# A two-layer streaming encoder step on one core: elementwise work moved from GpSimd to VectorE

## Chip, cores and metric

One NeuronCore of a Trainium2 chip runs the whole program. The metric is the device time of one execution in microseconds (us). PE is the matrix engine TensorE, DVE is VectorE, ACT is ScalarE, POOL is GpSimd, and SP is the engine that issues nearly all loads and stores.

## What is computed

The reference is a two-layer trunk with width 1024, run over 1024 prompt frames and 64 sample frames. Layer 0 mixes tokens with causal pooling windows, layer 1 with the gated linear recurrence HGRN2. Each layer ends in a convolutional feed-forward block, and an RMS norm closes the trunk. The feed-forward block, to which most of the change belongs, is this:

```python
up = jnp.einsum('bld,df->blf', h, w_up)
gate_pre, val = jnp.split(up, 2, axis=-1)
ext = jnp.concatenate([hist.astype(up.dtype), gate_pre], axis=1)
conv = cb
for j in range(CONV_W):
    conv = conv + cw[j] * ext[:, j:j + L]
hid = jax.nn.silu(conv.astype(F32)) * val.astype(F32)
y = jnp.einsum('blf,fd->bld', hid.astype(h.dtype), w_down)
```

and the trunk ends with `x = rmsnorm(x, norm_out_g)`. All inputs and outputs are float32. The hidden width is 2816, that is 22 blocks of 128.

## The kernel before

**Tiling.** The 1088 columns (frames) are three chunks: 384, 384 and 256 + 64 (the last 64 are the sample). Activations lie with 128 features on the partitions and frames along the free axis. The running sum x of each chunk stays in SBUF.

**Each product is three matmuls.** PE multiplies in a rounded format (F32R). Each operand is split into a high part, rounded by ACT, and a low part, the difference of the original and the high part. `mm3` (L181 to L185) adds hi x hi, hi x lo and lo x hi in a PSUM bank. `load_ready` (L112 to L133) loads a weight block of 128x512 through SP into one of five "raw" buffers, rounds it on ACT (L131) and makes the low part (L132) on the engine that `lo_engine` (L109) names: DVE in the HGRN part, for the pooling weights and for the first blocks of each feed-forward part (up blocks 0 to 3, down blocks 0 and 1), POOL for all others. There are eight places for the pairs of high and low part; when PE's last use of a place is issued, `drop` frees it and the next block is loaded. A raw buffer is free when its low part is made.

**Feed-forward.** Its 22 hidden blocks are done in 11 groups of two. The first group is computed plainly. From the second group on, chunks 0 and 1 are multiplied in Strassen's manner: seven products instead of eight, on sums and differences of weight parts (L155, on DVE) and of activations (`sums`, L426, on DVE). `Block.part` (L700) takes one of the products "3", "4", "1", "5", "2", "7", "6" at a time, and collects them: the partial sum e, the gate rows ge0 and ge1, and the values v0. Product "7" holds two subtractions on POOL, L727 and L730. `conv` (L618) does the three taps (L632 on ACT, L633 and L634 on DVE, SiLU at L635 on ACT), `hidden` (L638) multiplies by the values and splits the result. Chunk 2 is computed plainly (`plain`, L664). In the last group the plain blocks of chunk 2 come at the end, with parts named "upp". `down` (L752) multiplies two hidden blocks with the down weights, one PSUM bank for each of 8 output blocks and three chunks, and adds each bank to x (L760, on DVE). The down stage of a group runs inside the next group. There are three PSUM banks for the up products of chunks and chains and five for all else.

**Final norm.** `norm` (L356) with kind 3 squares x on ACT, adds up the squares on DVE and POOL (L369), sums over the partitions with PE transposes, takes the reciprocal root by Newton steps on DVE (`rstd`, L332 to L348), spreads it back into a PSUM bank by PE, copies that bank on ACT (L401), and multiplies x by it (L408): for chunks 0 and 1 on POOL, for chunk 2 on DVE but for two of eight. SP stores the output in pairs of blocks.

**Order.** PE's instruction order is written by hand (`manual_schedule`, L1087): Python generators are run by a small planner (`run`, L264) with estimated costs. For the other engines the framework orders the instructions when it builds the program. POOL besides does copies of two columns and fills (L625 to L628, L682, L684, L689, L722, L729, L732, L1013).

Of the kernel before, what the change touches and what calls it, by code (L numbers as in the profile page):

```python
# [9 lines left out]
F32 = mybir.dt.float32  # L10
# [55 lines left out]
def trunk_kernel(ctx: ExitStack, tc: tile.TileContext, xtok, xs_tok, hist_tok, xf, par, gmix, pw, winm, ident_in,  # L66
                 masks_in, w_up, w_dn, w_in, w_out, s0, y_out, npool, nhg, nconv):
    nc = tc.nc
# [37 lines left out]
    free = [(i, False) for i in range(NR)]  # L106
    extra_w = []

    def lo_engine(ph, key):  # L109
        return nc.vector if ph == "g" or key[0] == "pw" or key[0] in ("up", "dn") and key[2] < (4, 2)[key[0] == "dn"] else nc.gpsimd  # L110

    def load_ready(most=None):  # L112

        while queue and (most is None or len(loaded) < most):
            ph, key, make = queue[0]
            own = [p for p in free if p[1]] if ph == "g" and key[:2] not in (("out", H - 2), ("out", H - 1)) else []
            p = own[0] if own else next((p for p in free if not p[1]), None)
            if p is None:
                return
            free.remove(p)  # L120
            queue.pop(0)
            places[key] = p
            i, extra = p
            nm = "_".join(str(k) for k in key)
            if extra:
                hi, lo = (extra_w[i // 2][:, (i % 2 * 2 + b) * HW_:(i % 2 * 2 + b + 1) * HW_] for b in range(2))
            else:
                hi = wp.tile([P, HW_], F32R, name=f"whi{nm}", tag=f"whi{i}", bufs=1)
                lo = wp.tile([P, HW_], F32R, name=f"wlo{nm}", tag=f"wlo{i}", bufs=1)
            src = make(nm)  # L130
            nc.scalar.copy(hi, src)  # L131
            lo_engine(ph, key).tensor_tensor(lo, src, hi.bitcast(F32), op=ALU.subtract)  # L132
            loaded[key] = (hi, lo)  # L133

    def raw_block(nm, src, i):
# [190 lines left out]
    def slot(nm, tag, bufs=1, dt=F32, w=SLOT):  # L326
        return wk.tile([P, w], dt, name=nm, tag=tag, bufs=bufs)
# [28 lines left out]
    def norm(c, gbase, nm, kind):  # L356
# [5 lines left out]
        for d in range(ND):  # L362
            a = acc[d % 2][:, :n]
            if d < 2:
                nc.scalar.activation(a, x[c][:, d, :], AF.Square)
            else:
                sq = slot(f"sq_{nm}{d}", *tags[2:])
                last = nc.scalar.activation(sq[:, :n], x[c][:, d, :], AF.Square)
                (nc.vector if kind < 3 or c == 2 or d % 2 else nc.gpsimd).tensor_tensor(a, a, sq[:, :n], op=ALU.add)  # L369
        if final:  # L370
            with tc.issue_after(last.ins):
                for d in range(ND):
# [23 lines left out]
            yield 0.0, L_ROWS  # L396
        if kind == 0 and c == 0:
            nc.scalar.copy(piece("r0", *T1[6 + c], F32), pr[:, :n])
        if final:
            rs = slot(f"r_{nm}", "cv", 3)  # L400
            nc.scalar.copy(rs[:, :n], pr[:, :n])  # L401
        while kind == 2 and c < 2 and not last_proj:
            yield 0.0, 0.2
        for d in range(ND):
            if final:
                on_pool = c < 2 or d in (2, 5)
                eng, r_ = (nc.gpsimd, rs) if on_pool else (nc.vector, pr)
                eng.tensor_tensor(x[c][:, d, :], x[c][:, d, :], r_[:, :n], op=ALU.mult)  # L408

                if c < 2 and d % 2 or c == 2 and (d % 2 == 0 or d == ND - 1):  # L410
                    d0 = d - (0 < d and (c < 2 or d % 2 == 0))
                    nc.sync.dma_start(y_out[c][:, d0:d + 1, :], x[c][:, d0:d + 1, :])
            else:
                if kind == 2 and c < 2 or kind == 0 and c == 1:
                    t = row(kind // 2, c, d)
                elif kind == 0 and c < 2:
                    t = slot(f"hn_{nm}{d}", ("hh1", "hl1")[d % 2], 2, F32, NMAX)
                else:
                    t = slot(f"hn_{nm}{d}", "cv", 3)
                last = nc.vector.scalar_tensor_tensor(t[:, :n], x[c][:, d, :], col(gbase, d), pr[:, :n], op0=ALU.mult, op1=ALU.mult)  # L420
                split(hn_hi[c][:, d, :], hn_lo[c][:, d, :], t[:, :n], nc.vector)
                if d < ND - 1:
                    yield 0.0, N_STEP[kind]
# [189 lines left out]
    def ffn(l, hn_ready, late_deps, gbase, nm, kind):  # L613
# [82 lines left out]
        class Block:  # L696
# [3 lines left out]
            def part(self, t, keep=False):  # L700
# [22 lines left out]
                elif t == "2":  # L723
                    self.v0 = kept(f"v{nm}", "v", 2, ps)
                elif t == "7":
                    g0 = slot(f"g{nm}", "g", 1)[:, :N0]
                    nc.gpsimd.tensor_tensor(g0, self.e, self.ge1[:, 2:2 + N0], op=ALU.subtract)  # L727
                    ge0 = slot(f"ge{nm}_0", "ge", 3)
                    nc.gpsimd.memset(ge0[:, 0:2], 0.0)  # L729
                    nc.gpsimd.tensor_tensor(self.e, self.e, self.v0, op=ALU.subtract)  # L730
                    nc.vector.tensor_tensor(ge0[:, 2:2 + N0], g0, ps[:, :N0], op=ALU.add)
                    nc.gpsimd.tensor_copy(self.ge1[:, 0:2], ge0[:, N0:N0 + 2])  # L732
                    hidden(j, jj, 0, conv(j, 0, ge0), self.v0, hid)
                else:
                    nc.vector.tensor_tensor(self.e, self.e, ps[:, :N0], op=ALU.add)
                    hidden(j, jj, 1, conv(j, 1, self.ge1), self.e, hid)
# [446 lines left out]
```

## Time and profile before

| what | value |
|---|---|
| median of 3 runs | 2343.5 us (2336.83 to 2346.57) |
| profiled execution, its own time | 2341.33 us |
| its span, first to last instruction | 2339.5 us |
| mean granted TensorE clock in it | 0.988 of full |
| PE busy | 2269.2 us, 97% |
| DVE busy | 1621.5 us, 69% |
| ACT busy | 904.5 us, 39% |
| POOL busy | 755.1 us, 32% |
| bytes from HBM | 210.51 MB |

All times in the profile are of one execution; the runs shown beside it lie within 0.5% of each other. The page gives busy time for each engine, and the views of the trace break it down by stretch, by line and by wait. A busy engine is not the bound by itself: what matters is whose work PE, or the end of the program, waits for.

### The profile page before, as it was taken

The page shows a single profiled execution, that of the slowest core. Times are in us where ns is not written, and L with a number is a line of the kernel's source. Part 1 is how long each engine was busy: PE and PEld are TensorE (multiplying, and loading weights), DVE is VectorE, ACT ScalarE, POOL GpSimd, SP SyncE. Part 2 cuts the span into 40 slices and gives each one's busy share as a digit, 9 for nine tenths or more (in the row PEclk, how much of TensorE's full clock was granted, in tenths as well). Part 3 has the DMA queues.
Part 4 walks back from the last instruction along what each step waited for, and adds up shares of the span by engine and source line. Part 5 has one row for each costly group of instructions (what it writes and reads, how often), then busy time and mean ns, then how long its engine had stood idle before and what let it go on. Part 6 is the DMA issues. An engine that isn't in the chain of part 4 may idle for free.

```text
span 2339.5 us, 38021 instructions
## 1 busy us (share of the span) xinstructions
PE 2269.2 (97%) x13830; PEld 2219.9 (95%) x13830; DVE 1621.5 (69%) x3926; ACT 904.5 (39%) x1965; POOL 755.1 (32%) x856
## 2 busy tenths in 40 slices
PE   9899999999999989999999999989999999999996
PEld 8899999999999989999999999889999999999996
DVE  7896665666666698767666767788665666665667
ACT  6444433333443353323223322344433333444335
POOL 0024555455564500000000000001455455655555
PEclk9999999999999999999999999999999999999998
DMA  7124333334433321001001100102433333443331
GB/s 244 43 95 136 117 123 121 118 120 134 136 113 130 123 69 37 26 19 55 27 28 48 33 27 22 37 30 86 130 114 131 118 123 121 139 132 118 125 114 78
DMA packets 118099, 218.70 MB, mean 93 GB/s; under 512 B 13436, under 2 KB 17404, under 8 KB 117528
## 3 DMA queue, kind: packets, MB, share of 16 engines
q1 hardware_dynamic: 117822, 216.15, 28.7%
q8 instruction: 109, 1.79, 0.3%
q14 instruction: 78, 0.64, 0.1%
q10 hardware_dynamic: 90, 0.12, 0.0%
HBM read 210.51 MB, written 5.72 MB: 92 GB/s over the span
## 4 chain that ended last, share of the span: by engine, by line
PE 86%; DVE 7%; DMA 2%; ACT 2%; POOL 2%; issue 1%; SPq 0%; DVEq 0%; POOLq 0%; ACTq 0%
PE dn L183 7%; PE dn L184 6%; PE dn L185 6%; PE pj L183 6%; PE pj L185 5%; PE pj L184 5%; PE pz L184 3%; PE pz L185 3%; PE pz L183 3%; PE pl L948 3%; PE pv L183 2%; PE pg L183 2%; PE pv L184 2%; PE pv L185 2%; PE pg L185 2%; PE pg L184 2%
## 5 line engine op out<-in xcount | busy, mean ns | idle before, releaser
L132 POOL TENSOR_TENSOR wloup_a<-rawup_a,whiup_a 128x512 fp32r<-128x512 f32 x316 | 439.6, 1408 | 458.8 <-ACT whiup_a L131 428.7
L131 ACT CAST whiup_a<-rawup_a 128x512 fp32r<-128x512 f32 x368 | 224.4, 618 | 578.5 <-PE dn L184 397.1
L155 DVE TENSOR_TENSOR rawup_a<-rawup_a,rawup_a 128x512 f32<-128x512 f32 x200 | 184.5, 923 | 272.7 <-DMA rawup_a<-w_up_in 253.0
L183 PE MATMUL dn<-hh,whidn 128*128 128x384 f32 (+1 forms) x1056 | 351.6, 333 | 14.4 <-DVE x L760 9.5
L184 PE MATMUL dn<-hl,whidn 128*128 128x384 f32 (+1 forms) x1056 | 349.2, 331 | 0.5 <-DVE hl L189 0.5
L185 PE MATMUL dn<-hh,wlodn 128*128 128x384 f32 (+1 forms) x1056 | 349.3, 331 | 0.0
L760 DVE TENSOR_TENSOR x<-x,dn 128x384 f32<-128x384 f32 (+1 forms) x528 | 263.5, 529 | 101.6 <-PE dn L185 100.3
L183 PEld LDWEIGHTS dn<-hh,whidn 128*128 128x128 f32 x1056 | 200.6, 190 | 19.2 <-DVE x L760 13.6
L1013 POOL MEMSET gss<- 128x4 f32 x24 | 2.4, 101 | 633.5 <-DVE nt_g L336 633.5
L184 PEld LDWEIGHTS dn<-hl,whidn 128*128 128x128 f32 x1056 | 200.7, 190 | 1.0 <-DVE hl L189 1.0
L185 PEld LDWEIGHTS dn<-hh,wlodn 128*128 128x128 f32 x1056 | 200.6, 190 | 0.0
L183 PE MATMUL pj<-hnhi,whiin 128*128 128x384 f32 (+1 forms) x528 | 184.3, 349 | 0.0
L185 PE MATMUL pj<-hnhi,wloin 128*128 128x384 f32 (+1 forms) x528 | 172.6, 327 | 0.0
L184 PE MATMUL pj<-hnlo,whiin 128*128 128x384 f32 (+1 forms) x528 | 172.4, 326 | 0.0
L633 DVE SCALAR_TENSOR_TENSOR cv<-ge,prm,cv 128x322 f32<-128x322 f32 (+1 forms) x132 | 128.3, 973 | 45.0 <-ACT cv L632 41.4
L963 DVE COPY_PREDICATED at<-masks,pl 128x64 f32<-128x64 uint8 (+7 forms) x432 | 116.3, 294 | 32.1 <-PE pl L948 31.1
L132 POOL TENSOR_TENSOR wlodn<-rawdn,whidn 128x512 fp32r<-128x512 f32 x80 | 106.2, 1329 | 88.3 <-ACT whidn L131 83.1
L635 ACT ACTIVATE cv<-cv 128x322 f32<-128x322 f32 (+1 forms) x132 | 67.2, 509 | 154.1 <-DVE cv L634 153.8
L185 PE MATMUL pg<-hnhi,wloup_a 128*128 128x320 f32 (+1 forms) x384 | 121.6, 317 | 4.7 <-DVE wloup_a L132 4.7
L183 PE MATMUL pg<-hnhi,whiup_a 128*128 128x320 f32 (+1 forms) x384 | 121.7, 317 | 0.0
L183 PE MATMUL pv<-hnhi,whiup_a 128*128 128x320 f32 (+1 forms) x384 | 121.3, 316 | 0.0
L184 PE MATMUL pg<-hnlo,whiup_a 128*128 128x320 f32 (+1 forms) x384 | 121.2, 316 | 0.0
(1233 smaller groups left out, 6161.2 us busy)
## 6 DMA issues: line engine op xcount, KB each, us to landing
rawup_a<-w_up_in SPq DMA_DIRECT2D x568, 256.0 KB, 2.9
rawdn<-w_dn_in SPq DMA_DIRECT2D x88, 256.0 KB, 3.0
rawin<-w_in_in SPq DMA_DIRECT2D x64, 256.0 KB, 2.7
rawupp_a<-w_up_in SPq DMA_DIRECT2D x16, 256.0 KB, 2.8
rawout<-w_out_in SPq DMA_DIRECT2D x16, 256.0 KB, 2.6
xt<-xtok_in SPq DMA_DIRECT2D x7, 448.0 KB, 6.3
x<-xf_in SPq DMA_DIRECT2D x2, 1536.0 KB, 8.9
y_out<-x SPq DMA_DIRECT2D x8, 384.0 KB, 2.3
```

Source lines behind the costliest of these rows:

```text
L131: nc.scalar.copy(hi, src)
L132: lo_engine(ph, key).tensor_tensor(lo, src, hi.bitcast(F32), op=ALU.subtract)
L155: nc.vector.tensor_tensor(t[0], t[0], t[1], op=bs[2])
L183: nc.tensor.matmul(ps, w[0][:, wsl], a_hi, start=first, stop=False, skip_group_check=more)
L184: nc.tensor.matmul(ps, w[0][:, wsl], a_lo, start=False, stop=False, skip_group_check=more)
L185: nc.tensor.matmul(ps, w[1][:, wsl], a_hi, start=False, stop=last, skip_group_check=more)
L633: nc.vector.scalar_tensor_tensor(t[:, :wd], ge[:, 0:wd], prm[:, cw[0]:cw[0] + 1], t[:, :wd], op0=ALU.mult, op1=ALU.add)
L635: nc.scalar.activation(t[:, :wd], t[:, :wd], AF.Silu)
L760: nc.vector.tensor_tensor(x[c][:, d, :], x[c][:, d, :], pd[:, :n], op=ALU.add)
L948: nc.tensor.matmul(pls[-1][:w, i % 2 * MW:i % 2 * MW + 3 * w // 2], kk[:, o:o + w], mv, start=True, stop=True)
L963: nc.vector.copy_predicated(dst[:, :, :, d * hh:], mk, a)
L1013: nc.gpsimd.memset(ss[:, :4], 1.0)
```

## The change

The low part of every weight block, the two subtractions of product "7", all sums of squares and all output products are made on DVE. The choice of engine in `load_ready` and in `norm` goes, and with it ACT's copy of the spread reciprocal root: DVE reads it from its PSUM bank. POOL keeps its copies of two columns and its fills. No tile, buffer, load or matmul is added or removed.

```diff
-    def lo_engine(ph, key):
-        return nc.vector if ph == "g" or key[0] == "pw" or key[0] in ("up", "dn") and key[2] < (4, 2)[key[0] == "dn"] else nc.gpsimd
...
             nc.scalar.copy(hi, src)
-            lo_engine(ph, key).tensor_tensor(lo, src, hi.bitcast(F32), op=ALU.subtract)
+            nc.vector.tensor_tensor(lo, src, hi.bitcast(F32), op=ALU.subtract)
...
-                (nc.vector if kind < 3 or c == 2 or d % 2 else nc.gpsimd).tensor_tensor(a, a, sq[:, :n], op=ALU.add)
+                nc.vector.tensor_tensor(a, a, sq[:, :n], op=ALU.add)
...
-        if final:
-            rs = slot(f"r_{nm}", "cv", 3)
-            nc.scalar.copy(rs[:, :n], pr[:, :n])
...
             if final:
-                on_pool = c < 2 or d in (2, 5)
-                eng, r_ = (nc.gpsimd, rs) if on_pool else (nc.vector, pr)
-                eng.tensor_tensor(x[c][:, d, :], x[c][:, d, :], r_[:, :n], op=ALU.mult)
+                nc.vector.tensor_tensor(x[c][:, d, :], x[c][:, d, :], pr[:, :n], op=ALU.mult)
...
                     g0 = slot(f"g{nm}", "g", 1)[:, :N0]
-                    nc.gpsimd.tensor_tensor(g0, self.e, self.ge1[:, 2:2 + N0], op=ALU.subtract)
+                    nc.vector.tensor_tensor(g0, self.e, self.ge1[:, 2:2 + N0], op=ALU.subtract)
                     ge0 = slot(f"ge{nm}_0", "ge", 3)
                     nc.gpsimd.memset(ge0[:, 0:2], 0.0)
-                    nc.gpsimd.tensor_tensor(self.e, self.e, self.v0, op=ALU.subtract)
+                    nc.vector.tensor_tensor(self.e, self.e, self.v0, op=ALU.subtract)
```

## Rows read from the trace of the kernel before

**Rows 1.** The page's first part: engine, busy us, share of the span, instructions.

```profile
PE 2269.2 (97%) x13830; PEld 2219.9 (95%) x13830; DVE 1621.5 (69%) x3926; ACT 904.5 (39%) x1965; POOL 755.1 (32%) x856
```

**Rows 2.** Busy time by stretch; columns: stretch, length, engines, clock, DMA share, GB/s.

```profile
240.00:780.00 540.00, 534.74 (x3219) 532.28 (x3218) 340.87 (x541) 202.89 (x394) 293.09 (x315) 1.00 0.39 125
780.00:900.00 120.00, 109.99 (x636) 107.18 (x635) 96.82 (x244) 56.78 (x116) 27.69 (x32) 0.96 0.23 74
900.00:1500.00 600.00, 599.07 (x3799) 573.73 (x3799) 426.49 (x1659) 186.35 (x529) 2.23 (x22) 1.00 0.10 33
...
1680.00:2270.00 590.00, 586.95 (x3536) 584.89 (x3535) 368.63 (x591) 220.82 (x428) 322.22 (x343) 1.00 0.39 125
2270.00:2339.50 69.50, 50.14 (x286) 46.96 (x284) 51.96 (x108) 36.72 (x77) 38.13 (x42) 0.86 0.21 80
```

**Rows 3.** POOL's groups by form: busy us, mean ns, idle before and releasers.

```profile
L132 POOL TENSOR_TENSOR wloup_a<-rawup_a,whiup_a 128x512 fp32r<-128x512 f32 x316 | 439.6, 1408 | 458.8 <-ACT whiup_a L131 428.7 <-DVE e L716 25.5 <-DVE hl L189 4.3
L132 POOL TENSOR_TENSOR wlodn<-rawdn,whidn 128x512 fp32r<-128x512 f32 x80 | 106.2, 1329 | 88.3 <-ACT whidn L131 83.1 <-DVE hl L189 4.6
```

**Rows 4.** DVE's groups by form, the same columns.

```profile
L760 DVE TENSOR_TENSOR x<-x,dn 128x384 f32<-128x384 f32 x352 | 186.4, 550 | 65.9 <-PE dn L185 64.9
L155 DVE TENSOR_TENSOR rawup_a<-rawup_a,rawup_a 128x512 f32<-128x512 f32 x200 | 184.5, 923 | 272.7 <-DMA rawup_a<-w_up_in 253.0 <-issue 6.1 <-POOL ge L729 5.9
...
L633 DVE SCALAR_TENSOR_TENSOR cv<-ge,prm,cv 128x384 f32<-128x384 f32 x88 | 83.2, 947 | 38.2 <-ACT cv L632 35.6 <-POOL ge L732 1.3
L634 DVE SCALAR_TENSOR_TENSOR cv<-ge,prm,cv 128x384 f32<-128x384 f32 x88 | 72.4, 822 | 0.2
...
L132 DVE TENSOR_TENSOR wloin<-rawin,whiin 128x512 fp32r<-128x512 f32 x44 | 30.0, 690 | 3.7 <-ACT whiin L131 3.6
...
L420 DVE SCALAR_TENSOR_TENSOR hn_m<-x,prm,nr_m 128x384 f32<-128x384 f32 x16 | 9.5, 608 | 0.0
```

**Rows 5.** Busy time by stretch, columns as in Rows 2: one group's stages.

```profile
316.50:361.30 44.80, 44.80 (x273) 44.80 (x273) 28.34 (x42) 24.06 (x48) 33.16 (x37) 1.00 0.42 134
...
157.50:181.20 23.70, 23.70 (x145) 23.70 (x144) 17.46 (x35) 2.53 (x6) 0.00 (x0) 1.00 0.25 84
181.20:196.50 15.30, 14.81 (x83) 14.03 (x83) 15.14 (x28) 8.78 (x18) 2.32 (x3) 1.00 0.37 122
```

**Rows 6.** Waits: PE's from 240 to 790 us, DVE's of the span; us, times, longest.

```profile
PE dn L183 <- DVE x L760: 3.8, 4, 1.5
...
DVE rawup_a L155 <- DMA rawup_a<-w_up_in: 253.0, 120, 4.0
```

**Rows 7.** DVE's timeline in a down stage: start, us, instruction, idle before.

```profile
310.51 0.69 DVE L155 TENSOR_TENSOR rawup_a<-rawup_a,rawup_a 128x512 f32<-128x512 f32 x1 [2.17 <-DMA rawup_a<-w_up_in]
311.12 2.38 DVE L760 TENSOR_TENSOR x<-x,dn 128x384 f32<-128x384 f32 x5
```

**Rows 8.** DVE's timeline at the end, the same columns.

```profile
2305.97 1.32 DVE L189 TENSOR_TENSOR hl<-hr,hh 128x320 fp32r<-128x320 f32 x1 [0.83 <-ACT hh L188]
...
2310.12 0.92 DVE L347 SCALAR_TENSOR_TENSOR nt_o<-nt_o 128x3 f32<-128x3 f32 x1
2310.96 1.37 DVE L633 SCALAR_TENSOR_TENSOR cv<-ge,prm,cv 128x322 f32<-128x322 f32 x1
2312.37 1.17 DVE L634 SCALAR_TENSOR_TENSOR cv<-ge,prm,cv 128x322 f32<-128x322 f32 x1
...
2321.61 1.36 DVE L369 TENSOR_TENSOR acc_o<-acc_o,sq_o 128x320 f32<-128x320 f32 x1
...
2331.45 0.16 DVE L347 SCALAR_TENSOR_TENSOR nt_o<-nt_o 128x3 f32<-128x3 f32 x1
2333.20 2.48 DVE L408 TENSOR_TENSOR x<-x,nr_o 128x320 f32<-128x320 f32 x6 [1.59 <-ACT r_o L401]
```

**Rows 9.** POOL's timeline at the end, the same columns.

```profile
2306.90 8.45 POOL L408 TENSOR_TENSOR x<-x,r_o 128x384 f32<-128x384 f32 x8
```

**Rows 10.** PE's timeline at the end, the same columns.

```profile
2315.17 0.63 PE L183 MATMUL dn<-hh,whidn 128*128 128x320 f32 x1 [3.09 <-ACT hh L188]
```

## The prediction

> **What bounds the kernel.** I read the page's first part first. TensorE (PE) is busy 2269.2 of 2339.5 us, 97%; VectorE (DVE) 69%, GpSimd (POOL) 32% [rows 1]. So there are only 70.3 us in which PE does nothing, and a change that leaves PE's work alone can win no more than what it takes out of these. PE's order is written by hand, and the diff does not touch it.
>
> Next the busy time by stretch, to see where the 70 us lie [rows 2]. The two long feed-forward stretches, 240 to 780 and 1680 to 2270 us, have 5.3 and 3.1 us of idle PE (length minus PE's busy time). The hand-over between the layers (780 to 900) has 10.0, the end (2270 to 2339.5) 19.4. The HGRN part (900 to 1500) has 0.9, and POOL works only 2.2 us there: nothing moves in it. What is left of the 70 us, some 32, lies at the start and around 1500 to 1620 us, where the low parts are made on DVE already. The change can thus win in three places: 8.4 us in the feed-forward stretches, 10.0 at the hand-over, 19.4 at the end.
>
> **What moves, and its weight.** POOL makes 316 + 80 low parts of "up" and "down" weights [rows 3], and 16 more for the plain blocks of the last groups (4 parts x 2 blocks x 2 layers by the code). L727 and L730 run once in each block of ten groups of a layer (10 x 2 x 2 = 40 each): 80 subtractions. At the end 18 products (L408) and 6 sums (L369) move.
>
> On DVE a low part of this size takes 690 ns, and a 384-wide sum 550 ns [rows 4]: 412 x 0.690 = 284 us, 80 x 0.55 = 44, 24 x 0.55 = 13, together 341 us more for DVE. Some comes back: L155 has the shape of a low part but takes 923 ns, 233 more; L633 and L634 take 947 and 822 where an operation of their kind and shape at L420, run while POOL is quiet, takes 608 [rows 4]. That is 200 x 0.233 + 88 x 0.339 + 88 x 0.214 = 47 + 30 + 19 = 96 us. So DVE goes from 1621.5 to at most 1621.5 + 341 - 96 = 1866 us, 80% of the span. On the average it does not become the bound; the question is each stretch.
>
> **Feed-forward stretches.** A group of two blocks is an "up" stretch of 45 us and a "down" stretch of 24. In one up stretch (316.5 to 361.3) DVE is busy 28.3 of 44.8 us [rows 5]. POOL made 19 low parts there, so add 19 x 0.69 + 4 x 0.55 = 15.3, and take off some 3.8 (7 L155 and 8 of L633 and L634 at the excess above): 39.8 of 44.8 us. That is tight, but the trace has a preview: the low parts of the first two groups are made on DVE already. In the down stretch 157.5 to 181.2 PE is busy 23.70 of 23.70 us, and in 181.2 to 196.5, with DVE full (15.14 of 15.3 us, mixing sums on top), PE still has 14.81 of 15.3 [rows 5].
>
> What stalls PE now is mostly L760, the sum that empties a down bank: 3.8 us in 4 waits in layer 0 [rows 6]. It comes late because L155 stands in front of it in DVE's queue waiting for its load, 253 us in 120 waits over the span [rows 6]; behind one such wait five L760 run in one go [rows 7]. A load is started when a raw buffer (there are five) is free, that is when its low part is made. On POOL that takes 1.4 us and queues behind others, on DVE 0.69; so loads start sooner and these waits shrink. SP's queue gets no instruction more or less, and POOL's 2-column copies no longer queue behind low parts. What a low part waits for on DVE is ScalarE's rounding of the high part, right in front of it. PE's gain is at most 8.4 us; below, the loss has no end that a row gives, and I price it as the first rival. I take half of the gain, **-4**, because the preview's down stretch has no idle PE at all, while its full stretch loses 0.5 us.
>
> **Hand-over.** POOL works 27.7 us there, so DVE, 96.8 of 120 us busy [rows 2], gets some 14 more at half POOL's price and loses its contention. Between -3 (a third of PE's idle time) and +5, I take **0**: DVE's queue is full there with or without it.
>
> **The end.** Chunk 2's last block runs through DVE while POOL multiplies chunk 0's output (8 products from 2306.9, 8.45 us) [rows 9]. In that time the low part at 2305.97 takes 1.32 us and one of four Newton steps 0.92, the convolution steps 1.37 and 1.17, a sum at 2321.61 1.36 [rows 8]. Free of POOL, the 320-wide products at 2333.2 take 2.48/6 = 0.41 each and a Newton step 0.16 [rows 8]. These steps are in the chain in front of PE's wait of 3.09 us for the last hidden activations [rows 10]. Saved: 0.9 + 4 x 0.75 + (0.8 + 0.6, against 0.6 us at L420) + 0.9 = 6.2 us. Against it: chunk 2's last products are eight in a row instead of six beside two, 0.8 more, less the 0.4 of ScalarE's copy in front, which goes: +0.4. And 16 products of chunks 0 and 1 join DVE at 0.47 each (five sums in 2.38 us, [rows 7]), 3.8 us for each chunk. Hidden wholly, the end is worth -5.8; both in front of the chain, +1.7. Chunk 1's run beside the last down stage, chunk 0's half in gaps: **-4**. The output's PSUM bank is held for eight products instead of one copy; five banks cover that in a stage where PE waits anyway.
>
> **Sum.** -4 + 0 - 4 = -8 us on the profiled execution's 2341.3 us (1.8 over its span): 2333.3. The median of the three runs, 2343.5, lies 2.2 above that execution, so the forecast is **2335.5 us**, 0.34% less. About 0.5% (11.7 us) is what a measurement of this kernel can tell from no change.
>
> **Rivals.**
> First, slower: DVE becomes the bound in the up stretches. With 39.8 of 44.8 us of work it may idle 5 us in each; it idles 16.5 today [rows 5]. If more than 5 survive, DVE falls behind and L760 of the next down stage comes late. Half of 16.5 would be 3.2 us too much; if the down stage passes on half of that to PE, 18 stretches (nine groups, two layers) lose some 30 us, and the 4 us of gain are gone: 2335.5 + 4 + 30 = 2369. For it: the tightness. Against it: in the preview DVE has no waits left when it is late, since its inputs lie ready. The Trainium skill ("Perfetto Trace Analysis", Optimizing Scalar/DVE Operations) says that with a saturated DVE, handing work even to GPSIMD can make sense, though the port they share may spoil it; by the first half of that rule this change goes the wrong way, and by the second it does not. The trace bears out the second half (L155 at 923 against 690 ns) and shows saturation in the preview alone. Chance 0.2.
>
> Second, all DVE-made stalls go: -8.4 in the feed-forward stretches, -3 at the hand-over, -5.8 at the end: 2343.5 - 17 = 2326. For it: PE's waits there name L760 and chains through DVE. Against it: a DVE at 80% serves nothing at once. Chance 0.2.
>
> Third, nothing comes of it: the framework sets the order on DVE, and puts the output products in front of the last chain; the end then gives +1.7 and the feed-forward stretches break even: about 2345. Chance 0.1.
>
> **How the numbers follow.** The forecast has 0.5; of that I give 0.1 to gains beyond 11.7 us, as the end's bounds and half the stalls allow, and 0.4 to within it. Faster: 0.1 + 0.2 = 0.3; same: 0.4 + 0.1 = 0.5; slower: 0.2. The range goes from just under the second rival, 2324, through the third to a part of the first, 2356 (a hold-up of 1 us in each of 18 stretches, 18 us, on a forecast without the 4).
>
> **What would show it.** Right: DVE near 78 to 80% busy, POOL under 5%, L155 at 0.69 us and L633 at 0.61, fewer waits of L155 for loads, PE idle under 8 us in the two long stretches, and a wait for the last hidden activations that ends earlier after the last plain block. Wrong: PE idle grows in each up or down stretch with L760, L716 or a low part as the releaser, DVE without idle time in whole groups, or the last chain held by L408.

## The result and the profile after

The changed kernel takes 2331.87 us (median of 9 runs, 2323.85 to 2336.82), the kernel before beside it 2346.57 us (9 runs, 2336.83 to 2349.01): the ratio is 0.9935, 95% interval 0.992 to 0.9949. That is 0.65% less where 0.34% was forecast. The time lies in the range given, the sign is right, and the gain is just past the 0.5% that a measurement of this kernel can tell. The profiled execution of after takes 2332.14 us, with a span of 2330.4.

The page's first part after the change, to be read against [rows 1]:

```profile
PE 2272.7 (98%) x13830; PEld 2230.2 (96%) x13830; DVE 1773.2 (76%) x4442; ACT 911.8 (39%) x1962; POOL 122.1 (5%) x340
```

The same stretches as in [rows 2], after the change (stretch, length, then busy time of PE, weight loads, DVE, ACT, POOL, then clock, DMA share, GB/s):

```profile
240.00:780.00 540.00, 540.00 (x3264) 540.00 (x3263) 408.60 (x757) 207.24 (x396) 36.32 (x108) 1.00 0.39 125
780.00:900.00 120.00, 111.71 (x655) 109.60 (x654) 103.68 (x269) 58.96 (x121) 7.49 (x12) 0.97 0.23 74
...
1680.00:2270.00 590.00, 590.00 (x3564) 590.00 (x3564) 445.20 (x824) 227.77 (x434) 39.55 (x120) 1.00 0.39 126
2270.00:2330.40 60.40, 42.88 (x247) 40.85 (x245) 48.64 (x129) 30.51 (x65) 4.79 (x6) 0.85 0.20 77
```

In both long stretches PE now works without a gap: the 5.3 and 3.1 us of idle time are gone, all of them. Windows at fixed times can't tell how much shorter a stage became, so here are stretches between the same matmuls in both kernels. First the kernel before: from the start to the first matmul of Strassen's products in layer 0, from there to its last, from there to the first matmul of the HGRN part; then Strassen's products in layer 1, and what follows them.

```profile
0.00:140.50 140.50, 126.71 (x837) 122.54 (x838) 114.88 (x296) 79.61 (x165) 13.60 (x23) 0.98 0.40 127
140.50:809.20 668.70, 660.27 (x3970) 656.72 (x3970) 429.83 (x698) 252.49 (x491) 343.58 (x372) 1.00 0.39 125
809.20:844.20 35.00, 33.05 (x205) 32.31 (x204) 32.84 (x67) 20.77 (x44) 9.91 (x14) 1.00 0.26 77
...
1650.20:2274.00 623.80, 620.27 (x3729) 617.42 (x3729) 393.35 (x630) 240.96 (x466) 342.35 (x366) 1.00 0.39 126
2274.00:2339.50 65.50, 46.14 (x263) 42.96 (x262) 49.48 (x105) 33.68 (x72) 34.55 (x38) 0.86 0.20 77
```

The same five of the kernel after:

```profile
0.00:149.60 149.60, 136.70 (x837) 132.75 (x838) 115.43 (x296) 79.45 (x165) 13.14 (x23) 0.90 0.37 119
149.60:811.00 661.40, 658.25 (x3970) 657.14 (x3970) 504.94 (x939) 256.62 (x492) 45.25 (x132) 1.00 0.39 126
811.00:843.50 32.50, 32.50 (x205) 32.45 (x204) 30.82 (x72) 20.94 (x44) 5.78 (x8) 1.00 0.24 76
...
1648.40:2267.50 619.10, 618.61 (x3730) 617.83 (x3729) 469.83 (x870) 245.07 (x467) 42.87 (x127) 1.00 0.39 127
2267.50:2330.40 62.90, 45.38 (x263) 43.35 (x261) 51.14 (x134) 32.54 (x69) 5.55 (x8) 0.85 0.20 76
```

The two feed-forward stretches lose 7.3 and 4.7 us, the hand-over 2.5, the end 2.6; the parts not shown 1.1. That is 18.2 us. The start, in which the change moves nothing, took 9.1 us more at a lower clock (0.90 against 0.98). That is no effect of the change: e6_end_later (below), the same kernel up to its end, takes 139.7 us at 0.99 there. The nine runs of after fall into two groups some 8 us apart (four from 2323.85 to 2325.01 us, five from 2331.87), and the profiled one is of the slower group. So the stages gained about twice what the two spans show (9.1 us), and the medians (14.7 us) lie between.

What PE waits for L760, the sum that empties a down bank, in the kernel before, from 200 to 830 us, then from 1660 to 2290 (us in total, times, longest). After the change no such wait is left in the two feed-forward stretches.

```profile
PE dn L183 <- DVE x L760: 4.2, 5, 1.5
...
PE dn L183 <- DVE x L760: 1.8, 5, 0.7
```

DVE's groups by form in the kernel after, as in [rows 4] (L752 was L760, L152 was L155, L129 was L132, L625 and L626 were L633 and L634):

```profile
L129 DVE TENSOR_TENSOR wloup_a<-rawup_a,whiup_a 128x512 fp32r<-128x512 f32 x368 | 248.0, 687 | 54.7 <-ACT whiup_a L128 54.3
L752 DVE TENSOR_TENSOR x<-x,dn 128x384 f32<-128x384 f32 x352 | 190.4, 551 | 89.7 <-PE dn L182 89.2
L152 DVE TENSOR_TENSOR rawup_a<-rawup_a,rawup_a 128x512 f32<-128x512 f32 x200 | 137.7, 689 | 68.6 <-DMA rawup_a<-w_up_in 66.9 <-DVE ge L723 0.9
...
L626 DVE SCALAR_TENSOR_TENSOR cv<-ge,prm,cv 128x384 f32<-128x384 f32 x88 | 53.9, 613 | 0.1
L625 DVE SCALAR_TENSOR_TENSOR cv<-ge,prm,cv 128x384 f32<-128x384 f32 x88 | 53.7, 616 | 10.6 <-ACT cv L624 10.6
```

The weight mixing takes 0.69 us instead of 0.92, the convolution steps 0.61 instead of 0.95 and 0.82, and the mixing waits 66.9 us for its loads instead of 253.0 [rows 6].

The end is the one place that did not go as hoped. DVE's timeline there, then PE's (start, duration, instruction, in brackets the idle time before):

```profile
2294.64 3.33 DVE L400 TENSOR_TENSOR x<-x,nr_o 128x384 f32<-128x384 f32 x7
2298.00 0.49 DVE L186 TENSOR_TENSOR hl<-hr,hh 128x320 fp32r<-128x320 f32 x1
2298.41 0.55 DVE L400 TENSOR_TENSOR x<-x,nr_o 128x384 f32<-128x384 f32 x1
2298.87 0.55 DVE L373 TENSOR_TENSOR acc_o<-acc_o,acc_o 128x384 f32<-128x384 f32 x1
```

```profile
2299.48 0.90 PE L378 MATMUL nps_o<-ident,acc_o 128*128 128x128 f32 x3 [4.35 <-DVE acc_o L373]
...
2300.98 0.47 PE L180 MATMUL pg<-hnhi,whiupp_a 128*128 128x320 f32 x1
2301.25 0.47 PE L181 MATMUL pg<-hnlo,whiupp_a 128*128 128x320 f32 x1
...
2306.11 0.31 PE L181 MATMUL pv<-hnlo,whiupp_a 128*128 128x320 f32 x1
2306.26 0.31 PE L182 MATMUL pv<-hnhi,wloupp_a 128*128 128x320 f32 x1
...
2308.65 0.41 PE L180 MATMUL dn<-hh,whidn 128*128 128x320 f32 x1 [0.44 <-ACT hh L185]
```

Chunk 0's eight output products (L400) stand in DVE's queue in front of the sum L373 that PE needs for chunk 1's norm. PE idles 4.35 us. Its next matmuls start 0.27 us apart, at a granted clock of 0.50 from 2300.5 to 2305.0 us, which is the lower of its two levels (1.2 GHz), and are then back at 0.15 and 1.00. The wait for the last hidden activations, on the other hand, went from 3.09 us [rows 10] to 0.44, and 0.42 more for their low part. A part of that is only that PE came there late itself; e6_end_later (below) has the same place without the lateness.

### The profile page after: what moved, and what is told of

Its sections match the earlier page's. It is cut to its first block, busy times and chain, and to the rows that moved or that the text cites. A ratio compares the mean times of both kernels' runs of the same rounds, so it can differ in the third digit from the quotient of the medians.

```text
span 2330.4 us, 37924 instructions
## 1 busy us (share of the span) xinstructions
PE 2272.7 (98%) x13830; PEld 2230.2 (96%) x13830; DVE 1773.2 (76%) x4442; ACT 911.8 (39%) x1962; POOL 122.1 (5%) x340
## 3 DMA queue, kind: packets, MB, share of 16 engines
q8 instruction: 109, 1.79, 0.3%
## 4 chain that ended last, share of the span: by engine, by line
PE 91%; DVE 6%; ACT 1%; DMA 1%; issue 1%; SPq 0%; DVEq 0%; ACTq 0%
PE dn L181 7%; PE dn L182 7%; PE dn L180 7%; PE pj L180 6%; PE pj L182 5%; PE pj L181 5%; PE pz L181 4%; PE pz L182 4%; PE pz L180 4%; PE pl L940 3%; PE pg L180 3%; PE pg L182 3%; PE pg L181 2%; PE pv L180 2%; PE pv L181 2%; PE px L181 2%
## 5 line engine op out<-in xcount | busy, mean ns | idle before, releaser
L752 DVE TENSOR_TENSOR x<-x,dn 128x384 f32<-128x384 f32 (+1 forms) x528 | 273.8, 530 | 129.8 <-PE dn L182 128.1
L129 DVE TENSOR_TENSOR wloup_a<-rawup_a,whiup_a 128x512 fp32r<-128x512 f32 x368 | 248.0, 687 | 54.7 <-ACT whiup_a L128 54.3
L152 DVE TENSOR_TENSOR rawup_a<-rawup_a,rawup_a 128x512 f32<-128x512 f32 x200 | 137.7, 689 | 68.6 <-DMA rawup_a<-w_up_in 66.9
L182 PE MATMUL pv<-hnhi,wloup_a 128*128 128x320 f32 (+1 forms) x384 | 120.3, 313 | 0.0
L181 PE MATMUL pv<-hnlo,whiup_a 128*128 128x320 f32 (+1 forms) x384 | 120.3, 313 | 0.0
L180 PE MATMUL px<-hnhi,whiup_a 128*128 128x384 f32 x320 | 108.2, 338 | 3.7 <-DVE e L708 2.7
L181 PE MATMUL px<-hnlo,whiup_a 128*128 128x384 f32 x320 | 108.1, 338 | 0.8 <-DVE hnlo L186 0.7
```

The costliest lines, as they stand in the source:

```text
L129: nc.vector.tensor_tensor(lo, src, hi.bitcast(F32), op=ALU.subtract)
L152: nc.vector.tensor_tensor(t[0], t[0], t[1], op=bs[2])
L180: nc.tensor.matmul(ps, w[0][:, wsl], a_hi, start=first, stop=False, skip_group_check=more)
L181: nc.tensor.matmul(ps, w[0][:, wsl], a_lo, start=False, stop=False, skip_group_check=more)
L182: nc.tensor.matmul(ps, w[1][:, wsl], a_hi, start=False, stop=last, skip_group_check=more)
L752: nc.vector.tensor_tensor(x[c][:, d, :], x[c][:, d, :], pd[:, :n], op=ALU.add)
```

## Experiments

Two theories of the feed-forward gain were tried. **A**, the prediction's: POOL's slow low parts hold the five raw buffers, so loads start late, and the mixing that waits for a load blocks the sums that empty PE's banks. **B**: POOL's large operations stop DVE's own. The table has all runs; "mixing waits" is what the mixing instruction (L155 before, L152 after) waits for loads. Times are us; the ratio is to the kernel before, run beside each. Layer 0 and layer 1 are the two feed-forward stretches of one profiled execution. Up to the end e6_end_later gives every engine the same order as the change, and its layer 0 is 1.5 us longer; so a difference of that size in layer 0 says nothing.

| run | median | ratio (95%) | layer 0 | layer 1 | mixing waits | DVE busy | POOL busy |
|---|---|---|---|---|---|---|---|
| before | 2346.57 | | 668.7 | 623.8 | 253.0 | 1621.5 | 755.1 |
| after | 2331.87 | 0.9935 (0.992 to 0.9949) | 661.4 | 619.1 | 66.9 | 1773.2 | 122.1 |
| e1_low_only | 2333.48 | 0.9949 (0.9929 to 0.9968) | 662.9 | 619.1 | 83.2 | 1736.3 | 211.6 |
| e2_rest_only | 2337.38 | 0.9966 (0.9951 to 0.9982) | 664.0 | 623.3 | 153.6 | 1688.8 | 665.8 |
| e3_port_busy | 2496.1 | 1.0641 (1.0617 to 1.0666) | 737.4 | 692.9 | 34.2 | 2092.0 | 729.3 |
| e4_raw4 | 2328.7 | 0.993 (0.9905 to 0.9955) | 663.4 | 619.1 | 88.5 | 1772.1 | 123.6 |
| e9_raw3 | 2339.51 | 0.9988 (0.9974 to 1.0003) | 665.8 | 621.9 | 137.2 | 1762.7 | 103.1 |
| e8_port_private | 2465.15 | 1.0527 (1.0503 to 1.055) | 724.4 | 682.0 | 106.6 | 1951.0 | 735.4 |
| e11_port_half | 2333.74 | 0.9942 (0.9925 to 0.9959) | 664.9 | 621.0 | 107.8 | 1814.5 | 564.4 |
| e10_hold_only | 2388.07 | 1.0174 (1.0144 to 1.0203) | 691.1 | 646.7 | 179.7 | 1754.2 | 708.2 |
| e12_hold_half | 2332.53 | 0.9918 (0.989 to 0.9946) | 665.6 | 620.9 | 124.7 | 1767.2 | 531.3 |
| e5_dose1 | 2366.85 | 1.0104 (1.0073 to 1.0135) | 669.1 | 620.6 | 6.5 | 2016.0 | 188.9 |
| e5_dose2 | 2646.27 | 1.1279 (1.1239 to 1.1319) | 795.5 | 740.7 | 1.8 | 2298.8 | 152.0 |
| e6_end_later | 2324.5 | 0.9917 (0.9897 to 0.9937) | 662.9 | 619.1 | 65.1 | 1771.4 | 121.6 |

**One part alone.** The kernel before with only the low parts moved (e1_low_only), and with all but the low parts moved (e2_rest_only).

Against the kernel before, e1_low_only has this edit alone, and e2_rest_only has the whole change without it:

```diff
-            lo_engine(ph, key).tensor_tensor(lo, src, hi.bitcast(F32), op=ALU.subtract)
+            nc.vector.tensor_tensor(lo, src, hi.bitcast(F32), op=ALU.subtract)
```

> Only the low parts move to VectorE; the two subtractions of product 7 and the final norm stay on GpSimd as in the kernel before. The two feed-forward stretches (first px matmul to last pz matmul of a layer) take 668.3 and 623.5 us before, 661.0 and 618.7 after the whole change. Theory A (low parts on GpSimd hold the raw buffers, so loads come late, the weight mixing on VectorE waits for them and holds up the sums that empty PSUM): 661 and 619 within 1 us, since all low parts are quick; waits of the mixing for loads near the 67 us of after, not the 253 of before. Theory B (the two engines' shared port stretches VectorE's operations, and that delay is what TensorE feels): nearly the same, 1 to 2 us worse, since 80 subtractions still collide. Theory C (the two subtractions alone did it): 668 and 623. The end (last pz to the end) is 65.8 us before and 63.3 after: here 65 to 66 if the contention of the output products costs there, 2 us less if low parts were what collided. Ratio to before 0.993 to 0.997.

> The complement: the two subtractions and the final norm move, the low parts stay where they were before. Theories A and B: stretches as before, 668 and 623 (within 1.5 us), waits of the mixing for loads near 250 us. Theory C: 661 and 619. The end as after, about 63 us, if it is the norm's move that made it shorter. Ratio to before 0.998 to 1.000.

The low parts alone bring 10.5 of the 12.0 us of the two stretches (5.8 and 4.7), and 0.6 at the end. The rest alone was expected to leave the stretches alone, and took 4.7 us off layer 0 and 0.5 off layer 1; it also took 5.4 us off the end, where both together take 2.6 (PE waits 4.1 us there for the norm's sums, L376, and 7.3 for the same sums, L373, after the whole change). The two gains in the stretches overlap: 10.5 and 5.2 are more than 12.0. The miss on layer 0 fits A as well as B: without the 80 subtractions in POOL's queue a low part gets its turn sooner, and the mixing's waits fall to 153.6 us; it also meets POOL less, and takes 822 ns instead of 923.

**Fewer raw buffers.** The changed kernel with four (e4_raw4, below) and three (e9_raw3) raw buffers instead of five.

```diff
-NRAW = 5
+NRAW = 4
```

> The changed kernel with four raw buffers instead of five: loads start later, no port is busier. Theory A: the mixing's waits for loads rise again, to 150 us or more, waits of PE for the sums of the down stage come back, and the stretches lose 3 us or more each (664 to 670 and 622 to 626). Theory B: the stretches stay at 661 and 619, since VectorE's operations are as short as after the change.

> The changed kernel with three raw buffers instead of five; low parts on VectorE as in the change, GpSimd quiet. A load must now wait for two buffers less; four instead of five raised the waits of L152 for loads from 67 to 88 us without making the stretches longer. Theory A (late loads in front of L752 cost PE its time): the waits of L152 for loads rise to 250 us or more, where they were before the change, and the stretches go back to about 668 and 623 us, some 2340 us. Theory B (contention): whatever the waits for loads do up to 250 us, the stretches stay within 1 us of 663 and 619, about 2330 us.

With four buffers A's expectation fell; but the waits hardly grew (88.5 us), so four buffers were hardly scarcer than five, and the run says less than it was meant to. With three they grew to 137.2 us, and the stretches by 4.4 and 2.8 us, with POOL quiet: B's limit of 1 us fell, and A's direction holds at a smaller size. DVE's order differs a little between kernels with different numbers of buffers.

**POOL holds buffers, without large operations.** The changed kernel, in which POOL makes copies of two columns behind each low part's rounding, the last of them from the raw block: five copies in e10_hold_only (below), three in e12_hold_half (one in place of the loop's three). The order on PE, DVE, ACT and SP is that of the changed kernel.

```diff
             nc.vector.tensor_tensor(lo, src, hi.bitcast(F32), op=ALU.subtract)
+            if not (ph == "g" or key[0] == "pw" or key[0] in ("up", "dn") and key[2] < (4, 2)[key[0] == "dn"]):
+                nc.gpsimd.tensor_copy(scr, hi[:, :2].bitcast(F32))
+                for _ in range(3):
+                    nc.gpsimd.tensor_copy(scr, scr)
+                nc.gpsimd.tensor_copy(scr, src[:, :2])
```

> The changed kernel; for each low part that GpSimd made before the change, GpSimd makes five copies of two columns (0.35 us each by the copies it has now, some 1.7 us together): the first reads the rounded high part, the last the raw block. So GpSimd keeps each raw buffer about as long as its low part did before the change (1.41 us behind the rounding), but hardly touches SBUF. The order on the other engines is that of the changed kernel, and the same is computed. Theory A (holding the raw buffers is what made the loads late): waits of L152 for loads from 67 back to 200 us or more, feed-forward stretches back to about 667 and 622 us, time about 2342 us. Theory B (only GpSimd's large operations, which stop VectorE's, make VectorE and with it the freeing of buffers late): waits below 100 us, stretches within 1.5 us of 661 to 663 and 619, time about 2332 us.

> The run in which GpSimd holds the raw buffers by copies of two columns, with three copies instead of five (some 0.9 us behind the rounding instead of 1.6, about what VectorE's own low part takes). Five copies made the two stretches 691 and 647 us, and L152's counterpart waited 180 us for loads and 81 us for GpSimd's copies. If the harm lies in how long a buffer is held (theory A): with 0.9 us a buffer comes free hardly later than VectorE frees it, so waits of 80 to 140 us together and stretches of 662 to 668 and 619 to 624, about 2336 us. If it lies in something else that the copies do (their number, or a wait that they add on VectorE): three fifths of the harm, 679 and 636, about 2365 us. Theory B: stretches of the changed kernel, 661 and 619, 2332 us.

DVE's waits in the run with five copies, then PE's for the sum that empties a down bank, L759 (us in total, times, longest; L157 is the mixing):

```profile
DVE rawup_a L157 <- DMA rawup_a<-w_up_in: 179.7, 101, 4.6
DVE x L759 <- PE dn L187: 69.5, 150, 1.4
DVE rawup_a L157 <- POOL scr L133: 49.0, 28, 3.3
DVE rawup_a L157 <- POOL scr L131: 31.8, 13, 2.9
...
PE dn L185 <- DVE x L759: 39.2, 34, 3.7
```

The mixing runs at its free speed (692 ns), so POOL's copies don't slow it. But it waits 260 us in all (179.7 for loads, and 49.0 + 31.8 that the profile puts down to POOL's copies), as it did before the change (253.0), and the stretches grow by 29.7 and 27.6 us, for the most part through PE's waits for L759. Holding the buffers, without large operations, is thus enough to bring the old waits back; B's expectation fell. With three copies the mixing waits 124.7 us for loads, and the stretches grow by 4.2 and 1.8 us: A's numbers, and far from three fifths of the harm.

The harm with five copies is larger than the 12 us before the change, and the trace shows a reason: the copies did not hold a raw buffer as long as POOL's low part had, but longer. From the end of ACT's rounding to the end of the last instruction that reads the buffer (mean of the 396 "up" and "down" blocks of [rows 3]) it is 1.00 us after the change, 1.63 with three copies, 1.63 in e2_rest_only, 1.79 before and 3.42 with five copies. The two stretches together grow in the same order: by 0, 6.0, 6.8, 12.0 and 57.3 us. A second cost of the five copies is small: a convolution step waits 18.9 us (16 times) for the kernel's own copies of two columns, which now stand behind the five in POOL's queue.

**POOL works on SBUF, without holding buffers.** In e3_port_busy, the changed kernel, POOL multiplies each finished low part by ones, in place. In e8_port_private and e11_port_half, with four raw buffers, POOL squares a tile of its own instead (128x512 and 128x256), once for each low part. The order on PE, DVE, ACT and SP is that of the kernel each is compared with.

The edit of e3_port_busy, behind the low part under the condition above, then that of e8_port_private in the same place (in e11_port_half the tile is half as wide):

```diff
+                lo4 = lo.rearrange("p (a b) -> p a b", b=P)
+                nc.gpsimd.tensor_tensor(lo4, lo4.bitcast(F32), warm.unsqueeze(1).to_broadcast([P, 4, P]), op=ALU.mult)
...
+                nc.gpsimd.tensor_copy(scr[:, :2], lo[:, :2].bitcast(F32))
+                nc.gpsimd.tensor_tensor(scr, scr, scr, op=ALU.mult)
```

> The changed kernel, with one more operation on GpSimd for each low part that GpSimd made before: it multiplies the finished low part by ones in place, the same size with two inputs from SBUF. So GpSimd is as busy as before (some 570 us more) and collides with VectorE as often, and PE waits for GpSimd's end as before; but the raw buffer is freed by VectorE's low part already. Theory A: the stretches stay near 661 and 619 (within 2 us), and the mixing's waits for loads stay under 110 us, although its mean duration goes back to 0.9 us. Theory B: the stretches go back to 668 and 623 or longer, as the collisions are all there and VectorE has more to do than before.

> The changed kernel with four raw buffers (as in the run before this one), and for every low part that GpSimd made before the change, GpSimd copies two columns of the finished low part into a 128x512 tile of its own and squares that tile. GpSimd thus works on SBUF as long as it did before the change (about 412 x 1.4 us), but holds no raw buffer and nothing of PE's or VectorE's waits for it. Computed is the same. Theory A (raw buffers held by GpSimd's slow low parts made the loads late): nothing changes against the kernel with four raw buffers: feed-forward stretches 663 and 619 us, L152 0.69 us, about 2329 us. Theory B (GpSimd working on SBUF stretches VectorE's own instructions): L152 and L625 at 0.9 us and more, stretches back to 667 to 669 and 622 to 624, about 2338 us. If the multiplies are far dearer than the low parts were, as in the run where they worked in place on the low part (stretches 737 and 693), the port alone does it.

> The run with the squares in a tile of GpSimd's own, with squares half as wide (128x256): four raw buffers, nothing held. The full squares made VectorE busy 179 us more and the two stretches 61 and 63 us longer than the same kernel without them. Theory B in proportion: half of it, some 90 us more of VectorE and about 30 us for each stretch, about 2395 us. If the harm has a threshold (VectorE has idle time to give as long as it is not full): 90 us more of VectorE, which is what it lost to GpSimd before the change (96 us by the prediction), and stretches only 5 to 8 us longer, about 2340 us. Theory A: nothing, 2329 us.

POOL's timeline of e8_port_private, then DVE's in the same stretch:

```profile
288.46 1.40 POOL L132 TENSOR_TENSOR scr<-scr 128x512 f32<-128x512 f32 x1
...
290.40 1.04 POOL L132 TENSOR_TENSOR scr<-scr 128x512 f32<-128x512 f32 x1
...
292.64 1.31 POOL L132 TENSOR_TENSOR scr<-scr 128x512 f32<-128x512 f32 x1
```

```profile
288.88 1.40 DVE L727 TENSOR_TENSOR e<-e,v 128x384 f32<-128x384 f32 x1
290.20 0.54 DVE L728 TENSOR_TENSOR ge<-g,pz 128x384 f32<-128x384 f32 x1
290.66 1.33 DVE L129 TENSOR_TENSOR wlodn<-rawdn,whidn 128x512 fp32r<-128x512 f32 x1
...
292.97 1.39 DVE L631 SCALAR_TENSOR_TENSOR cv<-ge,prm,cv 128x384 f32<-128x384 f32 x1
...
305.65 0.69 DVE L155 TENSOR_TENSOR rawup_a<-rawup_a,rawup_a 128x512 f32<-128x512 f32 x1 [3.35 <-DMA rawup_a<-w_up_in]
```

DVE's low part at 290.66 begins 0.26 us after POOL's square, and ends at 291.99, 0.55 us after the square's end at 291.44: it stands until POOL is through, then does its work. L631 at 292.97 ends 0.41 us after the square that ran when it began. L728, which reads one operand from PSUM, keeps its 0.54 us (542 ns on the mean of 40, where L727, with two operands in SBUF, takes 864; 552 each in the changed kernel). By the Trainium skill ("SBUF — State Buffer", Who interferes with whom) a DVE instruction with two SBUF inputs and a GpSimd instruction that reads SBUF exclude each other, and the second blocks fully; the trace agrees. A DVE that is late frees raw buffers late (1.70 us behind the rounding, where e4_raw4 has 1.00), and at 305.65 it waits 3.35 us for a load in turn: B ends in the place that A names.

With full squares both stretches grow by 61 and 63 us. With half of them POOL still works 332 us on its tile, and DVE loses 42 us, but the stretches grow by 1.5 and 1.9 only. So the harm is no proportion of POOL's work. Nor is it that DVE ran full, as layer 0 shows, first in e8_port_private, then in e5_dose1 of the next test (columns as in [rows 2]):

```profile
145.90:870.30 724.40, 678.41 (x3970) 670.18 (x3970) 589.11 (x937) 247.99 (x493) 340.50 (x528) 0.97 0.35 115
...
156.50:825.60 669.10, 661.55 (x3969) 659.84 (x3970) 615.64 (x1157) 252.92 (x490) 78.73 (x131) 0.99 0.38 125
```

With full squares DVE is busy 589 of 724 us and PE is idle for 46; with extra work of its own DVE is busy 616 of 669 us and PE is idle for 8. The mixing waits for loads 106.6 us in the first and 6.5 in the second. Where between half and full squares the harm sets in, and why so steeply, was not tried. In the in-place run (e3), where PE must besides wait for POOL's result, the stretches grew by 76.0 and 73.8 us against the changed kernel, though the mixing waited only 34.2 us for loads: A's expectation fell there. Whether DVE's lateness or that of the low parts did it, this run can't tell.

**More work for DVE.** The changed kernel with one and two more instructions of the same size behind each feed-forward low part, which change no value: the first rival by itself (the framework orders ACT's queue a little differently here). The loop runs once in e5_dose1 (below) and twice in e5_dose2.

```diff
             nc.vector.tensor_tensor(lo, src, hi.bitcast(F32), op=ALU.subtract)
+            for _ in range(1 if ph == "f" else 0):
+                nc.vector.tensor_tensor(lo, lo.bitcast(F32), lo.bitcast(F32), op=ALU.max)
```

> The changed kernel with one more VectorE instruction of the same size, which changes nothing in value, behind each of the feed-forward low parts (476 x 0.69 = 328 us more for VectorE, 2101 us or 90% of the span). In the feed-forward stretches VectorE is busy about 45 of 60 us now and would be at 62 of 60. If VectorE's queue serves PE in time until it is full (its sheer work is the bound): the stretches lengthen by 2 of 60, 22 and 20 us, about 2374 us. If half of its idle time can't be used, as the first rival of the prediction had it: 69 of 60, some 100 us for each stretch, above 2500 us. If VectorE can be late without PE noticing: below 2345 us.

> The changed kernel with two more VectorE instructions of the same size behind each feed-forward low part. One of them made VectorE busy 243 us more (0.53 us each, since in a full queue one begins before the one before it ends) and 55 of 60 us in the feed-forward stretches, where PE had no idle time. With two it would have 65 of 60 us to do: if its sheer work is the bound from there on, the stretches lengthen by a twelfth, some 55 and 50 us on 669 and 621, about 2480 us. If the bound comes from queueing, more than that; if the stretches can share their work out, less than 2420 us.

The feed-forward stretches of e5_dose1 by windows of 60 us (columns as above), then of e5_dose2:

```profile
300.00:360.00 60.00, 60.00 (x367) 60.00 (x367) 54.02 (x102) 22.26 (x43) 8.83 (x14) 1.00 0.37 119
360.00:420.00 60.00, 60.00 (x360) 60.00 (x359) 55.18 (x106) 21.45 (x42) 7.89 (x9) 1.00 0.37 119
```

```profile
240.00:300.00 60.00, 49.03 (x280) 47.96 (x279) 55.09 (x104) 16.55 (x32) 3.12 (x7) 0.91 0.32 104
300.00:360.00 60.00, 49.71 (x296) 49.10 (x295) 59.29 (x109) 23.23 (x45) 5.65 (x14) 0.92 0.37 119
```

With one more, DVE works 54 and 55 of 60 us in these windows and PE still does not wait; layer 1 grows by 1.5 us and layer 0 by 7.7. Of the 32.6 us that the span is longer than the changed kernel's, 6.9 lie in the start, 7.0 in the hand-over, 7.7 between the HGRN part and layer 1's Strassen products, and 3.5 at the end. The total was forecast well (2374), the place was not. With two more, DVE is all but full (55 and 59 of 60 us), PE waits 185.2 us in 21 times for the sum that empties its banks, and the granted clock falls to 0.92: 2646 us where sheer work would have made 2480. From there on the price is above what the sum of DVE's work explains; how it divides between the queue's order and the clock was not tried.

**A later place for the output products.** The changed kernel, in which the products of chunks 0 and 1 are held back until the next chunk's sums are issued.

```diff
+    summed = set()
...
+        if final:
+            summed.add(c)
...
+        while final and c < 2 and c + 1 not in summed:
+            yield 0.0, 0.2
```

> The changed kernel, with the output products of chunks 0 and 1 held back until the sums of the next chunk's norm are issued, so that chunk 0's eight products no longer stand in front of chunk 1's sum (L373) in VectorE's queue. If that order is what costs PE 4.35 us there, and the lower clock behind it (some 16 matmuls at 0.267 instead of 0.147 us, 1.9 us): the last stretch goes from 62.9 to about 57 us, and the time to about 2326 us. If the chain at the end is held by something else (the products then only come later, in front of the last ones): 62 to 64 us, about 2332 us.

DVE's timeline at the end of this kernel, and its last stretch:

```profile
2286.80 0.55 DVE L374 TENSOR_TENSOR acc_o<-acc_o,acc_o 128x384 f32<-128x384 f32 x1
2287.27 1.01 DVE L405 TENSOR_TENSOR x<-x,nr_o 128x384 f32<-128x384 f32 x2
```

```profile
2259.60:2316.50 56.90, 42.71 (x264) 40.63 (x262) 50.18 (x134) 32.78 (x69) 5.70 (x8) 0.92 0.22 85
```

The sum now stands ahead of the products, and the end takes 56.9 us instead of 62.9, at a mean clock of 0.92 instead of 0.85, as expected. Against the kernel before the ratio is 0.9917 (0.9897 to 0.9937). That is the lowest of the table, but its interval overlaps with that of the change, and e12_hold_half, whose stretches are longer, has 0.9918: whole times don't rank versions this close. The stretch does, and shows where the 6 us come from.

## Why the prediction was right, and where not

**The cap.** That the low parts stall PE through the mixing's waits held: the waits fell by three quarters, PE's waits for L760 are gone, and its idle time from 240 to 780 and from 1680 to 2270 us went to nothing. The step that failed is a size: "I take half of the gain, -4". Between the same matmuls the idle time fell by 8.3 us (5.3 and 3.0; 3.6 are left), and 3.7 us more came out of what counts as busy: 3970 matmuls of layer 0 are busy 660.27 us before and 658.25 after at the same clock. So the feed-forward term was -12.0. "PE's gain is at most 8.4 us" was wrong, since the ends of matmuls are modelled: in the last rows of PE above each is drawn 0.31 us long and the next starts 0.15 us later. A stall shorter than the difference isn't seen as idle time, and a longer one shows by that much too short.

**Why loads were late.** "L155 stands in front of it in DVE's queue waiting for its load" is borne out. In nine of the kernels the two stretches together follow the mixing's waits, whatever made them: 1282.0 us at 65.1, 1280.5 at 66.9, 1282.0 at 83.2, 1282.5 at 88.5, 1285.9 at 107.8, 1286.5 at 124.7, 1287.7 at 137.2, 1287.3 at 153.6, 1292.5 at 253.0 (e6, after, e1, e4, e11, e12, e9, e2, before). The sum of the waits is not the price, though: e10 has 1337.8 at 260 with POOL's copies, e8 1406.4 at 106.6, e3 1430.3 at 34.2, e5_dose1 1289.7 at 6.5. The prediction gave holding as the only cause of the late loads, and contention as a cost of DVE's time alone. The runs show that each can do harm. How the 12 us divide between the two isn't shown, as in the kernel before the same instruction did both. But holding by itself would do: on a line between the runs with three and five copies (6.0 us more at 1.63 us of holding, 57.3 at 3.42) the 1.79 us of the kernel before come to 11 us, by estimate. Contention without holding cost the stretches 3.4 us where it took 42 us of DVE's time (e11); what the 95 us that it took before the change would cost alone was not tried.

**DVE's load.** "At most 1866 us" was 1773. The 96 us that come back are there, 46.8 in L155 and 48.0 in L633 and L634. Other forms gave back more, which the prediction left out: the 320-wide low parts of activations went from 1078 to 491 ns (25.8 us), the 322-wide L633 from 1026 to 553 (20.7). The rest is in part that DVE's instructions overlap when queued: the added ones were priced one by one, except the output products.

**The hand-over**, taken at 0, gave 2.5 us: PE's idle time between the two parts went from 1.95 us to none.

**The end**, taken at -4, gave -2.6. The savings on the last chain came, as e6_end_later shows, where PE is not late: it waits 1.33 us for a Newton step and 0.69 for the low part of the last hidden activations there, where the kernel before waits 2.37 for the Newton step and 3.09 for the activations. (One of the savings, 0.9 for the sum at 2321.61, lies behind that chain, not in it.) But "chunk 0's half in gaps" failed: its products stood in front of chunk 1's sum, for 4.35 us of PE and the clock behind it. This is the third rival's mechanism, one chunk earlier. Without it the end is worth -8.6 (65.5 to 56.9), more than the -5.8 of the bound.

**The rivals.** The first (DVE the bound) was off by far: with 243 us more on DVE the feed-forward stretches still cost 9 us in all. The second (all stalls go) was right for the feed-forward stretches in kind, and its 8.4 us were 12.0; its time of 2326 is nearest to the 2324.5 of e6_end_later. The third had the end's fault, and not its price. The upper end of the range was added up wrongly: 2335.5 + 4 + 18 is 2357.5, not 2356. The likeliest class, within 0.5%, was missed by little; the terms' sum of -8 stands beside 18.2 us less behind the start, or 14.7 in the medians. That the forecast of 2335.5 lies only 3.6 us from the measured time is thus in part luck: it started from a median of three runs, 2343.5, where nine gave 2346.57, and two errors had opposite signs, the end's gain too large by 1.4 us and the feed-forward gain too small by 8.0.

## What to carry to other kernels

When a slow engine holds a buffer that a load waits for, look for the price at the far end of the chain: here in the sums that stand behind the waiting mixing in another engine's queue. A move between engines has two effects, the held buffer and the blocked instructions, and small instructions with the same dependencies, or large ones with none, tell them apart, if the trace is then asked how long the small ones really held it: here five copies held it nearly twice as long as they were meant to. After such a move, read which instructions that nobody waits for now stand ahead of one that the bound engine needs; holding these back took 6.0 us off the end, a third of what the change took off behind the start.

## What was not expected of the hardware

- Queued DVE instructions overlap. In e5_dose1 two low parts in a row take 1.29 us, and the next instruction begins 1.20 us after the first: 0.60 each where one alone takes 0.69.

```profile
361.27 1.29 DVE L129 TENSOR_TENSOR wloup_a<-rawup_a,whiup_a 128x512 fp32r<-128x512 f32 x2
362.47 1.29 DVE L131 TENSOR_TENSOR wloup_a<-wloup_a 128x512 fp32r<-128x512 f32 x2
```

  476 more of them made DVE 243 us busier, 0.51 each. For a long queue the Trainium skill ("Vector Engine (DVE) Microarchitecture Reference", Measured stream behaviour on trn2) states 1.0417 ns for a column and some 75 ns for an instruction, an estimate of 0.61 us for 512 columns; the trace agrees.
- In e8_port_private POOL's square of 128x512 took 1.04 us where it was not delayed and up to 1.60 where it was, and the DVE instruction beside it up to more than twice its own time (L631 1.39 against 0.61 in the changed kernel).
- A fifth raw buffer is worth next to nothing once DVE makes the low parts: four gave 0.993 (0.9905 to 0.9955) against 0.9935.
